# Gate and up projections as 2x2 blocks, every second chunk with seven products instead of eight

## The chip, the cores and the metric

One core of a Trainium2 chip runs the whole kernel. The metric is the device time of one execution in microseconds. The profile shows one such execution: TensorE as PE (matmuls) and PEld (its weight loads), VectorE as DVE, ScalarE as ACT, GpSimd as POOL, and the queue of SyncE, which issues most loads, as SPq.

## The reference

A decoder trunk of two layers over 256 tokens (two tiles of 128) and a model width of 2048, all in float32. Layer 0 mixes by retention and a short convolution, layer 1 by differential attention. After each mixer comes the feed-forward part, which is what the change touches:

```python
def swiglu(h, w_gate, w_up, w_down):
    return (jax.nn.silu(h @ w_gate) * (h @ w_up)) @ w_down
...
x = x + swiglu(rms_norm(x, norm_ffn[layer]), ffn_w_gate[layer], ffn_w_up[layer], ffn_w_down[layer])
```

`w_gate` and `w_up` are 2048 x 5632, `w_down` is 5632 x 2048. The gain of the norm is a column factor of `h`; its row scale `r` is applied to the products' results.

## The kernel before

Each float32 product is made of three products in a reduced format, fp32r. A matrix `a` is split in `a_hi` (rounded to fp32r) and `a_lo = a - a_hi`; then `a @ w` is `a_hi w_hi + a_lo w_hi + a_hi w_lo`. The activation stands still in TensorE (128 k-rows by 128 tokens), the weights move through it (128 k-rows by 512 columns), and one PSUM bank holds 128 tokens by 512 columns.

`col_block` (L126) makes one block of 512 columns for both token tiles. It loads the weights with SPq in pieces of four k-tiles, 1 MB each, into the tag `raw` (four buffers, L131), and goes through them in chunks of KC = 2 k-tiles: ScalarE makes `whi` (L138), VectorE `wlo` (L140), both of four buffers in the pool `wpool`, and TensorE runs 12 matmuls per chunk (2 token tiles x 2 k-tiles x 3, L146 to L148), each with its own weight load. A block over 16 k-tiles is 96 matmuls.

`ffn` (L398) runs three parts of 4, 4 and 3 column blocks. A block calls `col_block` for gate, lets ScalarE apply silu (L408), calls it for up, multiplies on VectorE (L411), and leaves a job that turns the hidden block for the down projection (`split4`, L158: four transposes on TensorE, `hi` on ScalarE at L165, `lo` on VectorE at L166). `step` (L114), called after every chunk, runs one piece of the oldest job, so jobs are spread through the next block. After each part, `out_proj` (L390) multiplies with the rows of `w_down` and adds to the residual `x_sb` (L228). There are 11 such gate and up pairs in each of the two layers, 22 in all.

`Stream` holds a norm's activation: `pair` (L184) turns two k-tiles of the residual and splits them (L197, L198); `part` runs it as a job while the projection ahead goes on.

The program's order and the tiles' dependencies are written out; `TileContext(nc, schedule_with_timeline_sim=True)` then fixes, before launch, the order of the instructions on each engine. Each engine runs its own list strictly in that order, waiting on semaphores. SPq and GpSimd's queue are two such lists.

Of the kernel before, what the change touches and what calls it, by code (L numbers as in the profile page):

```python
# [9 lines left out]
F32 = mybir.dt.float32  # L10
F32R = mybir.dt.float32r
# [24 lines left out]
def decoder_trunk(ctx: ExitStack, tc: tile.TileContext, a: dict):  # L36
# [16 lines left out]
    ident = cpool.tile([P, P], F32, name="ident")  # L53
    x_sb = cpool.tile([P, NT, D], F32, name="x_sb")
    gcol = cpool.tile([P, 88], F32, name="gcol")
# [48 lines left out]
    def rsqrt_mean(out, ss, n):  # L104
        """out = (ss / n + eps) ** -0.5 on small [P, w] tiles."""
        w = ss.shape[1]
        nc.vector.tensor_scalar(out, ss, 1.0 / n, EPS, ALU.mult, ALU.add)
        nc.gpsimd.tensor_tensor(out, out, mhalf[:, :w], ALU.pow)

    # Work that follows a product but holds the tensor engine runs between the chunks of the next  # L110
    # product: each job is a generator that yields where the tensor engine should go on meanwhile.
    jobs = deque()

    def step():  # L114
# [9 lines left out]
            step()  # L124

    def col_block(name, w, row0, n0, nk, hi, lo, kd=KD):  # L126
        """acc[t] = act[t] @ w[row0 : row0 + nk * P, n0 : n0 + NB], act split in hi + lo."""
        acc = [acc_tile(f"{name}_a{t}") for t in range(NT)]
        for c0 in range(0, nk, KC):
            if c0 % KD == 0:  # L130
                raw = wpool.tile([P, KD, NB], F32, tag="raw", name=f"{name}_raw{c0}", bufs=4)  # L131
# [19 lines left out]
        return acc  # L151

    def act_pair(nk, tag, name):
        hi = apool.tile([P, nk, S], F32R, tag=tag + "h", name=name + "_hi")
        lo = apool.tile([P, nk, S], F32R, tag=tag + "l", name=name + "_lo")
        return hi, lo

    def split4(src, hi, lo, k0, t, name):  # L158
        """Transpose src [P tokens, 512] of token tile t into k-tiles k0 .. k0+3 of hi and lo."""
        pt = tp_tile(f"{name}_tp")  # L160
        for j in range(4):
            nc.tensor.transpose(pt[:, j * P : (j + 1) * P], src[:, j * P : (j + 1) * P], ident)
        pv = pt.rearrange("p (j s) -> p j s", j=4)
        ts = slice(t * P, (t + 1) * P)
        nc.scalar.copy(hi[:, k0 : k0 + 4, ts], pv)  # L165
        nc.vector.tensor_tensor(lo[:, k0 : k0 + 4, ts], pv, hi.bitcast(F32)[:, k0 : k0 + 4, ts], ALU.subtract)  # L166

    class Stream:
        """The residual stream's next normed activation: x * gain, transposed and split, with
        the row scale kept apart for the products' results."""  # L170

        def __init__(self, name, g0):
            self.name, self.g0 = name, g0
            self.hi, self.lo = act_pair(KT, "xT", name)
            self.ss = small.tile([P, NT, 4], F32, tag="ss", name=name + "_ss")
            self.r = small.tile([P, NT], F32, tag="r", name=name + "_r")
# [5 lines left out]
                nc.scalar.activation(junk, x_sb[:, t, cs], AF.Square, accum_out=self.ss[:, t, c : c + 1])  # L182

        def pair(self, q):  # L184
            """k-tiles 2q and 2q + 1."""
            pt = tp_tile(f"{self.name}_tp{q}")
            for j in range(2):
                k = 2 * q + j
# [4 lines left out]
            for j in range(2):  # L193
# [5 lines left out]
                    self.lo[:, k], pv, g, self.hi.bitcast(F32)[:, k], op0=ALU.mult, op1=ALU.subtract  # L199
                )  # L200

        def scale(self):
            s1 = small.tile([P, NT], F32, tag="s1", name=self.name + "_s1")
            nc.vector.reduce_sum(s1, self.ss, axis=AX.X)
            rsqrt_mean(self.r, s1, D)

        def part(self, c):
            yield
            self.pair(2 * c)
            self.pair(2 * c + 1)  # L210
            yield
            self.squares(c)
            if c == 3:
                self.scale()
# [13 lines left out]
            nc.vector.tensor_tensor(x_sb[:, t, cs], acc[t], x_sb[:, t, cs], ALU.add)  # L228

    def rope(psum_in, r, cos, sin, out, h, hd, name):  # L230
        """out = rope(r * in) for h heads of hd columns; sin's first half carries the minus."""
        half = hd // 2
        v = psum_in.rearrange("p (h d) -> p h d", d=hd)
        ca = work.tile([P, h, hd], F32, tag="ropeA", name=name + "_A")
# [10 lines left out]
        nc.gpsimd.tensor_tensor(out.rearrange("p (h d) -> p h d", d=hd), ca, cb, ALU.add)  # L245

    def transpose4(src, dst, t, name):
        """src [P tokens, 512] -> dst[:, 0:4, tokens of t], float32."""
        pt = tp_tile(f"{name}_tp")
        for j in range(4):  # L250
            nc.tensor.transpose(pt[:, j * P : (j + 1) * P], src[:, j * P : (j + 1) * P], ident)
        nc.scalar.copy(dst[:, :, t * P : (t + 1) * P], pt.rearrange("p (j s) -> p j s", j=4))
# [136 lines left out]
    def out_proj(name, w, nk, hi, lo, g0, row0=0, stream=True):  # L389
        nxt = Stream(name, g0) if stream else None  # L390
        for c in range(4):
            acc = col_block(f"{name}o{c}", w, row0, c * NB, nk, hi, lo)
            add_residual(acc, c)
            if nxt:
                jobs.append(nxt.part(c))
        return (nxt, nxt.r) if nxt else None

    def ffn(layer, st, r, after):  # L398
        wg, wu, wd = a["ffn_w_gate"][layer], a["ffn_w_up"][layer], a["ffn_w_down"][layer]
        res = None  # L400
        for part, (b0, b1) in enumerate(((0, 4), (4, 8), (8, 11))):
            hi, lo = act_pair(KT, "act", f"h{layer}{part}")
            for b in range(b0, b1):
# [8 lines left out]
                jobs.append(splits(gs, hi, lo, 4 * (b - b0), f"h{layer}{b}"))  # L412
            nk, row0 = 4 * (b1 - b0), b0 * NB
            if part < 2:
                out_proj(f"d{layer}{part}", wd, nk, hi, lo, 0, row0, stream=False)
            elif after is not None:
# [53 lines left out]
    scale = AD ** -0.5  # L470

    def rotary(i, nm, acc, grp):
        """Norm and rotary embedding of four heads' q or k; returns both token tiles."""
        ct, sn = tabs[i]
        rots = []
        for t in range(NT):
# [174 lines left out]
```

## Time and profile before

| | us |
|---|---|
| median of three runs | 2235.31 (2234.86 to 2235.60) |
| span of the profiled execution, first to last instruction | 2233.8 |
| busy in it: TensorE, VectorE, ScalarE, GpSimd | 2224.0, 1235.7, 996.0, 115.8 |
| loaded and stored by DMA | 418.90 MB, 188 GB/s over the span |

The page gives no time of its own for the profiled execution beyond its span. The span ends 1.5 us short of the median of the runs, and this is what lies around it. A matmul's row lasts from its start to its modelled end, and the next one starts before that: time per matmul is read from start to start, not from the durations.

### The profile page before, as it was taken

How to read it: one execution, taken by the hardware profiler on the slowest of the kernel's cores; microseconds unless marked ns; L12 is line 12 of the kernel's file. 1: busy time of each engine (PE TensorE's matmuls, PEld its weight loads, DVE VectorE, ACT ScalarE, POOL GpSimd, SP SyncE). 2: the span in 40 equal slices, each digit the busy share in tenths (PEclk: the TensorE clock that was granted, in tenths of full speed). 3: DMA queues.
4: the chain of work that ended last, by engine and by line, in shares of the span. 5: the costliest groups of instructions: out<-in, count | busy, mean ns of one | idle time of the engine just before them, and what ended most of it. 6: DMA issues, size and time to landing. Idle time of an engine off the chain costs nothing.

```text
span 2233.8 us, 25353 instructions
## 1 busy us (share of the span) xinstructions
PE 2224.0 (100%) x10115; PEld 1842.8 (82%) x10115; DVE 1235.7 (55%) x1320; ACT 996.0 (45%) x1172; POOL 115.8 (5%) x104
## 2 busy tenths in 40 slices
PE   8999999999999999999999999999999999999999
PEld 7888888888888888888888888888888888888887
DVE  5555565544554555455677778665445544554554
ACT  5444445444334443444545545554444344434443
POOL 1110000000000000000031233000000000000000
PEclk9999999999999999999999999999999999999999
DMA  8555555555565655555555555555555656555553
GB/s 286 174 180 188 191 186 188 189 189 189 189 197 192 193 190 188 189 189 188 188 177 164 188 170 170 170 188 189 189 189 189 194 190 193 191 192 189 188 188 132
DMA packets 212860, 418.90 MB, mean 188 GB/s; under 512 B 7341, under 2 KB 10885, under 8 KB 212613
## 3 DMA queue, kind: packets, MB, share of 16 engines
q1 hardware_dynamic: 209904, 414.34, 56.7%
q10 hardware_dynamic: 2836, 2.93, 0.4%
q8 instruction: 79, 1.29, 0.2%
q14 instruction: 41, 0.33, 0.0%
HBM read 415.15 MB, written 2.10 MB: 187 GB/s over the span
## 4 chain that ended last, share of the span: by engine, by line
PE 99%; DMA 1%; ACT 0%; DVE 0%; SPq 0%; issue 0%
PE g_a L146 7%; PE g_a L148 7%; PE g_a L147 7%; PE u_a L146 7%; PE u_a L147 7%; PE u_a L148 7%; PE av_a L148 1%; PE av_a L146 1%; PE ak_a L148 1%; PE n3o_a L147 1%; PE ak_a L147 1%; PE n3o_a L146 1%; PE aq_a L147 1%; PE aq_a L148 1%; PE n3o_a L148 1%; PE n1o_a L148 1%
## 5 line engine op out<-in xcount | busy, mean ns | idle before, releaser
L140 DVE TENSOR_TENSOR u_lo<-u_raw,u_hi 128x1024 fp32r<-128x1024 f32 x176 | 215.6, 1225 | 263.0 <-ACT u_hi L138 263.0
L140 DVE TENSOR_TENSOR g_lo<-g_raw,g_hi 128x1024 fp32r<-128x1024 f32 x176 | 215.6, 1225 | 226.5 <-ACT g_hi L138 224.8
L138 ACT CAST g_hi<-g_raw 128x1024 fp32r<-128x1024 f32 x176 | 185.5, 1054 | 287.3 <-PE g_a L147 139.9
L138 ACT CAST u_hi<-u_raw 128x1024 fp32r<-128x1024 f32 x176 | 185.6, 1055 | 252.0 <-PE u_a L147 132.9
L146 PE MATMUL g_a<-g_hi,n_hi 128*128 128x512 f32 x704 | 277.3, 394 | 0.0
L148 PE MATMUL g_a<-g_lo,n_hi 128*128 128x512 f32 x704 | 274.4, 390 | 0.0
L147 PE MATMUL g_a<-g_hi,n_lo 128*128 128x512 f32 x704 | 273.9, 389 | 0.0
L146 PE MATMUL u_a<-u_hi,n_hi 128*128 128x512 f32 x704 | 273.9, 389 | 0.0
L147 PE MATMUL u_a<-u_hi,n_lo 128*128 128x512 f32 x704 | 273.9, 389 | 0.0
L148 PE MATMUL u_a<-u_lo,n_hi 128*128 128x512 f32 x704 | 273.9, 389 | 0.0
L148 PEld LDWEIGHTS g_a<-g_lo,n_hi 128*128 128x128 f32 x704 | 132.1, 188 | 28.1
L148 PEld LDWEIGHTS u_a<-u_lo,n_hi 128*128 128x128 f32 x704 | 132.2, 188 | 27.5
L146 PEld LDWEIGHTS u_a<-u_hi,n_hi 128*128 128x128 f32 x704 | 132.2, 188 | 27.4
L147 PEld LDWEIGHTS u_a<-u_hi,n_lo 128*128 128x128 f32 x704 | 132.2, 188 | 27.4
L147 PEld LDWEIGHTS g_a<-g_hi,n_lo 128*128 128x128 f32 x704 | 132.3, 188 | 26.5
L146 PEld LDWEIGHTS g_a<-g_hi,n_hi 128*128 128x128 f32 x704 | 132.2, 188 | 26.2
L140 DVE TENSOR_TENSOR d11o_lo<-d11o_raw,d11o_hi 128x1024 fp32r<-128x1024 f32 x32 | 39.2, 1225 | 42.2 <-ACT d11o_hi L138 42.1
L140 DVE TENSOR_TENSOR d00o_lo<-d00o_raw,d00o_hi 128x1024 fp32r<-128x1024 f32 x32 | 39.2, 1225 | 42.2 <-ACT d00o_hi L138 42.1
L140 DVE TENSOR_TENSOR d01o_lo<-d01o_raw,d01o_hi 128x1024 fp32r<-128x1024 f32 x32 | 39.2, 1225 | 42.2 <-ACT d01o_hi L138 42.1
L140 DVE TENSOR_TENSOR d10o_lo<-d10o_raw,d10o_hi 128x1024 fp32r<-128x1024 f32 x32 | 39.2, 1225 | 42.2 <-ACT d10o_hi L138 42.1
L140 DVE TENSOR_TENSOR n1o_lo<-n1o_raw,n1o_hi 128x1024 fp32r<-128x1024 f32 x32 | 39.4, 1232 | 35.6 <-ACT n1o_hi L138 35.6
L138 ACT CAST d10o_hi<-d10o_raw 128x1024 fp32r<-128x1024 f32 x32 | 33.8, 1055 | 53.3 <-PE d10o_a L147 46.6
(305 smaller groups left out, 4594.1 us busy)
## 6 DMA issues: line engine op xcount, KB each, us to landing
g_raw<-in_ffn_w_gate_dram SPq DMA_DIRECT2D x88, 1024.0 KB, 5.2
u_raw<-in_ffn_w_up_dram SPq DMA_DIRECT2D x88, 1024.0 KB, 5.2
n1o_raw<-in_hyb_w_out_dram SPq DMA_DIRECT2D x16, 1024.0 KB, 5.1
d00o_raw<-in_ffn_w_down_dram SPq DMA_DIRECT2D x16, 1024.0 KB, 5.1
d01o_raw<-in_ffn_w_down_dram SPq DMA_DIRECT2D x16, 1024.0 KB, 5.1
aq_raw<-in_diff_w_qkv_dram SPq DMA_DIRECT2D x16, 1024.0 KB, 5.1
ak_raw<-in_diff_w_qkv_dram SPq DMA_DIRECT2D x16, 1024.0 KB, 5.1
av_raw<-in_diff_w_qkv_dram SPq DMA_DIRECT2D x16, 1024.0 KB, 5.1
```

Source lines behind the costliest of these rows:

```text
L138: nc.scalar.copy(whi, part)
L140: nc.vector.tensor_tensor(wlo, part, whi.bitcast(F32), ALU.subtract)
L146: nc.tensor.matmul(acc[t], lhsT=hi[:, k, ts], rhs=whi[:, j], start=first, stop=False)
L147: nc.tensor.matmul(acc[t], lhsT=lo[:, k, ts], rhs=whi[:, j], start=False, stop=False)
L148: nc.tensor.matmul(acc[t], lhsT=hi[:, k, ts], rhs=wlo[:, j], start=False, stop=last)
```

## The change

Gate and up are computed together. The four k-tiles of a chunk are halves k1 and k2, the tokens are tiles t0 and t1, and gate and up are the two halves of the columns: a 2x2 block product. `pair_blocks` loads x (gate, four k-tiles) and y (up). In chunks 1 and 3 (kind 8) it makes eight half products of 6 matmuls; two of them use the difference of the two token tiles in place of one tile, so that the results land in the same banks. In chunks 0 and 2 (kind 7) it makes seven, of sums of blocks: an accumulating DMA issued by GpSimd adds the gate half w11 to the loaded up half w12 (that is t1), VectorE makes t2 = t1 + w22, t3 = t2 - w11 (in place of w11) and t4 = t2 + w21 (in place of w21), and all seven operands are split. The sums of the activation are made once per layer in `quad`. Seven PSUM banks hold the products; VectorE and ScalarE put gate and up together from them behind each pair. To make room, the transposes have one bank (`tpb`) instead of two while a pair runs, the working tiles live in a pool that is closed and opened again by stage (`Phase`), and `raw` has six buffers instead of four in the feed-forward stages.

```diff
+    class Phase:
+        def begin(self, name, raw):
+            if self.close is not None:
+                self.close.close()
+            self.close = ExitStack()
+            self.pool = self.close.enter_context(tc.tile_pool(name=name, bufs=2, reuse_waits="tile"))
+            self.raw = raw
...
+        def raw_tile(self, name):
+            return self.pool.tile([P, KD, NB], F32, tag="raw", name=name, bufs=self.raw)
...
     def tp_tile(name):
-        return psum.tile([P, NB], F32, tag="tp", name=name, bufs=2)
+        tp_turn[0] ^= 1
+        tag = "tpa" if tp_turn[0] and tp_both[0] else "tpb"
+        return psum.tile([P, NB], F32, tag=tag, name=name, bufs=1)
...
+    def split_w(src, name):
+        whi = wpool.tile([P, KC, NB], F32R, tag="whi", name=name + "_hi")
+        nc.scalar.copy(whi, src)
+        wlo = wpool.tile([P, KC, NB], F32R, tag="wlo", name=name + "_lo")
+        nc.vector.tensor_tensor(wlo, src, whi.bitcast(F32), ALU.subtract)
+        return whi, wlo
+
+    def pair_blocks(name, wa, wb, n0, st):
...
+        b7 = psum.tile([P, NB], F32, tag="tpa", name=f"{name}_p7", bufs=1)
+        b35 = psum.tile([P, 2, NB], F32, tag="sc", name=f"{name}_p35")
...
+        def product(c, bank, act, w, last=True):
+            hi, lo = act
+            whi, wlo = w
+            for j in range(KC):
...
+                nc.tensor.matmul(acc, lhsT=hi[:, j], rhs=whi[:, j], start=first, stop=False)
+                nc.tensor.matmul(acc, lhsT=lo[:, j], rhs=whi[:, j], start=False, stop=False)
+                nc.tensor.matmul(acc, lhsT=hi[:, j], rhs=wlo[:, j], start=False, stop=end)
+
+        for c, kind in enumerate(kinds):
+            k0 = c * KD * P
+            x = work.raw_tile(f"{name}_x{c}")
+            y = work.raw_tile(f"{name}_y{c}")
...
+            nc.sync.dma_start(x, wa[rows, cols].rearrange("(k p) n -> p k n", p=P))
+            nc.sync.dma_start(y, wb[rows, cols].rearrange("(k p) n -> p k n", p=P))
+            w11, w21, w12, w22 = x[:, 0:KC], x[:, KC:KD], y[:, 0:KC], y[:, KC:KD]
...
+            if kind == 7:
+                half = slice(k0, k0 + KC * P)
+                nc.gpsimd.dma_start(w12, wa[half, cols].rearrange("(k p) n -> p k n", p=P), accum_op=ALU.add)
+                t1 = w12
+                product(c, "b1", a["a11"], split_w(w11, nm + "w11"))
+                product(c, "b2", a["a12"], split_w(w21, nm + "w21"))
+                step()
+                t2 = work.tile([P, KC, NB], F32, tag="t2", name=nm + "t2", bufs=1)
+                nc.vector.tensor_tensor(t2, t1, w22, ALU.add)
+                nc.vector.tensor_tensor(w11, t2, w11, ALU.subtract)
+                nc.vector.tensor_tensor(w21, t2, w21, ALU.add)
+                product(c, "b6", a["s2"], split_w(t2, nm + "t2"))
+                product(c, "b7", a["s3"], split_w(w11, nm + "t3"))
+                step()
+                product(c, "b4", a["a22"], split_w(w21, nm + "t4"))
+                product(c, "b5", a["s1"], split_w(t1, nm + "t1"))
+                step()
+                product(c, "b3", a["s4"], split_w(w22, nm + "w22"))
+                if c == seven[-1]:
+                    u2 = work.tile([P, NB], F32, tag="u2", name=name + "u2", bufs=1)
+                    nc.scalar.copy(u2, b1)
+                    nc.vector.tensor_tensor(u2, b6, u2, ALU.subtract)
+                    u3 = work.tile([P, NB], F32, tag="u3", name=name + "u3", bufs=1)
+                    nc.vector.tensor_tensor(u3, b7, u2, ALU.add)
+            else:
+                w = split_w(w11, nm + "w11")
+                product(c, "b2", a["a11"], w, False)
+                product(c, "b4", a["a21"], w, False)
+                step()
...
+            step()
+        flush()
...
+        def quad(self, c):
...
+            nc.scalar.copy(self.hi[:, ks], xg)
+            nc.vector.tensor_tensor(self.lo[:, ks], xg, self.hi.bitcast(F32)[:, ks], ALU.subtract)
...
+            if n == 4:
+                nc.vector.tensor_tensor(d[:, 0], xg[:, k1, t1], xg[:, k2, t1], ALU.subtract)
+                nc.vector.tensor_tensor(d[:, 2], xg[:, k1, t1], xg[:, k1, t0], ALU.subtract)
+                nc.vector.tensor_tensor(d[:, 1], xg[:, k2, t1], d[:, 2], ALU.subtract)
+                nc.vector.tensor_tensor(d[:, 3], xg[:, k2, t0], d[:, 1], ALU.subtract)
+            else:
+                nc.vector.tensor_tensor(
+                    d.rearrange("p i k s -> p (i k) s"), xg[:, :, t0], xg[:, :, t1], ALU.subtract
+                )
...
+            nc.scalar.copy(hi, d)
+            nc.vector.tensor_tensor(lo, d, hi.bitcast(F32), ALU.subtract)
...
         def part(self, c):
             yield
-            self.pair(2 * c)
-            self.pair(2 * c + 1)
+            if self.kinds:
+                self.quad(c)
...
     def ffn(layer, st, r, after):
...
-                acc = col_block(f"g{layer}{b}", wg, 0, b * NB, KT, st.hi, st.lo)
+                b1, b2, b3, b4, b5, u2, u3 = pair_blocks(f"f{layer}{b}", wg, wu, b * NB, st)
...
+                nc.scalar.copy(gs[0], b1)
+                nc.vector.tensor_tensor(gs[0], b2, gs[0], ALU.add)
+                nc.vector.tensor_tensor(gs[1], b4, u3, ALU.subtract)
                 for t in range(NT):
-                    nc.scalar.activation(gs[t], acc[t], AF.Silu, scale=r[:, t : t + 1])
-                acc = col_block(f"u{layer}{b}", wu, 0, b * NB, KT, st.hi, st.lo)
-                for t in range(NT):
-                    nc.vector.scalar_tensor_tensor(gs[t], acc[t], r[:, t : t + 1], gs[t], op0=ALU.mult, op1=ALU.mult)
...
+                    nc.scalar.activation(gs[t], gs[t], AF.Silu, scale=r[:, t : t + 1])
+                nc.vector.tensor_tensor(u3, b5, u3, ALU.add)
+                nc.vector.tensor_tensor(u2, b5, u2, ALU.add)
+                nc.vector.tensor_tensor(u2, b3, u2, ALU.add)
+                for t, u in enumerate((u2, u3)):
+                    nc.vector.scalar_tensor_tensor(gs[t], u, r[:, t : t + 1], gs[t], op0=ALU.mult, op1=ALU.mult)
...
+    KINDS = (7, 8, 7, 8)
+    st, r = out_proj("n1", a["hyb_w_out"][0], KT, ca_hi, ca_lo, 32, kinds=KINDS, begin=("ffn0", 6))
     st, r = ffn(0, st, r, 16)
+    work.begin("mix1", 4)
```

`out_proj` calls `work.begin` behind its first column block where `begin` is given, so the pool changes at three places: in the projection ahead of each feed-forward part (`ffn0`, `ffn1`) and behind the first feed-forward part (`mix1`).

## Rows read from the trace of the kernel before

**Rows 1.** The page's first and second part: busy time, and tenths in 40 slices.

```profile
PE 2224.0 (100%) x10115; PEld 1842.8 (82%) x10115; DVE 1235.7 (55%) x1320; ACT 996.0 (45%) x1172; POOL 115.8 (5%) x104
...
PEclk9999999999999999999999999999999999999999
```

**Rows 2.** The chain that ended last, by engine and by line.

```profile
PE 99%; DMA 1%; ACT 0%; DVE 0%; SPq 0%; issue 0%
PE g_a L146 7%; PE g_a L148 7%; PE g_a L147 7%; PE u_a L146 7%; PE u_a L147 7%; PE u_a L148 7%; PE av_a L148 1%; PE av_a L146 1%; PE ak_a L148 1%; PE n3o_a L147 1%; PE ak_a L147 1%; PE n3o_a L146 1%; PE aq_a L147 1%; PE aq_a L148 1%; PE n3o_a L148 1%; PE n1o_a L148 1%
```

**Rows 3.** Timeline of TensorE: start us, duration us, line, operation; first pair of blocks.

```profile
405.10 0.39 PE L146 MATMUL u_a<-u_hi,n_hi 128*128 128x512 f32 x1
...
426.86 0.39 PE L146 MATMUL g_a<-g_hi,n_hi 128*128 128x512 f32 x1
...
432.07 0.39 PE L148 MATMUL g_a<-g_lo,n_hi 128*128 128x512 f32 x1
432.31 0.60 PE L162 MATMUL h_tp<-ident,gs 128*128 128x128 f32 x4
...
432.97 0.39 PE L147 MATMUL g_a<-g_hi,n_lo 128*128 128x512 f32 x1
```

**Rows 4.** Groups by line: engine, tile, shapes, count, busy us, mean ns, idle before.

```profile
L140 DVE TENSOR_TENSOR u_lo<-u_raw,u_hi 128x1024 fp32r<-128x1024 f32 x176 | 215.6, 1225 | 263.0 <-ACT u_hi L138 263.0
L138 ACT CAST u_hi<-u_raw 128x1024 fp32r<-128x1024 f32 x176 | 185.6, 1055 | 252.0 <-PE u_a L147 132.9 <-PE g_a L147 119.1
L411 DVE SCALAR_TENSOR_TENSOR gs<-u_a,n_r,gs 128x512 f32<-128x512 f32 x44 | 32.3, 748 | 0.0
L166 DVE TENSOR_TENSOR h_lo<-h_tp,h_hi 128x512 fp32r<-128x512 f32 x44 | 30.1, 683 | 0.0
L228 DVE TENSOR_TENSOR x_sb<-d00o_a,x_sb 128x512 f32<-128x512 f32 x8 | 5.5, 688 | 0.1
L408 ACT ACTIVATE gs<-g_a,n_r 128x512 f32<-128x512 f32 x44 | 30.2, 687 | 11.3 <-PE g_a L148 11.2
```

**Rows 5.** Busy by stretch: us, PE, PEld, DVE, ACT, POOL, PEclk, DMA share, GB/s.

```profile
0.00:40.00 40.00, 34.22 (x150) 26.88 (x151) 22.18 (x33) 24.61 (x46) 1.84 (x10) 1.00 0.93 324
...
382.00:560.00 178.00, 178.00 (x802) 147.50 (x801) 89.59 (x85) 78.31 (x86) 0.70 (x1) 1.00 0.59 190
```

**Rows 6.** Timeline of VectorE around a change of block; in brackets the idle time.

```profile
425.20 1.23 DVE L140 TENSOR_TENSOR g_lo<-g_raw,g_hi 128x1024 fp32r<-128x1024 f32 x1 [1.50 <-ACT g_hi L138]
426.34 1.47 DVE L411 SCALAR_TENSOR_TENSOR gs<-u_a,n_r,gs 128x512 f32<-128x512 f32 x2
427.92 1.23 DVE L140 TENSOR_TENSOR g_lo<-g_raw,g_hi 128x1024 fp32r<-128x1024 f32 x1
...
433.36 1.23 DVE L140 TENSOR_TENSOR g_lo<-g_raw,g_hi 128x1024 fp32r<-128x1024 f32 x1 [1.50 <-ACT g_hi L138]
434.50 0.68 DVE L166 TENSOR_TENSOR h_lo<-h_tp,h_hi 128x512 fp32r<-128x512 f32 x1
```

**Rows 7.** DMA issues: tile, queue, count, KB each, median us to landing.

```profile
g_raw<-in_ffn_w_gate_dram SPq DMA_DIRECT2D x88, 1024.0 KB, 5.2
...
rq_raw<-in_hyb_w_in_dram SPq DMA_DIRECT2D x8, 512.0 KB, 7.6
```

**Rows 8.** Timeline of VectorE in the attention layer, beside GpSimd's work.

```profile
1142.73 0.69 DVE L486 TENSOR_TENSOR aqsb<-aqsb,aqrr 128x512 f32<-128x512 f32 x1
1143.45 0.69 DVE L489 TENSOR_TENSOR aqA<-aqsb,rtab 128x512 f32<-128x512 f32 x1
1144.32 1.22 DVE L486 TENSOR_TENSOR aqsb<-aqsb,aqrr 128x512 f32<-128x512 f32 x1 [0.17 <-POOL aqrr L108]
1145.47 1.76 DVE L140 TENSOR_TENSOR ak_lo<-ak_raw,ak_hi 128x1024 fp32r<-128x1024 f32 x1
```

**Rows 9.** Timeline of GpSimd in the same stretch.

```profile
1144.26 4.71 POOL L491 TENSOR_TENSOR aqB<-aqsb,rtab 128x256 f32<-128x256 f32 x4
```

More of the change, by code (lines that the diff above doesn't have):

```diff
@@ L130, in col_block @@
             if c0 % KD == 0:
-                raw = wpool.tile([P, KD, NB], F32, tag="raw", name=f"{name}_raw{c0}", bufs=4)
+                raw = work.raw_tile(f"{name}_raw{c0}")
             if c0 % kd == 0:
@@ L151, in col_block @@
         return acc
+    def split_w(src, name):
[5 more added lines that the diff above has]
+    def pair_blocks(name, wa, wb, n0, st):
+        b1 = acc_tile(f"{name}_p1")
+        b2 = acc_tile(f"{name}_p2")
+        b6 = acc_tile(f"{name}_p6")
+        b4 = acc_tile(f"{name}_p4")
+        b7 = psum.tile([P, NB], F32, tag="tpa", name=f"{name}_p7", bufs=1)
+        b35 = psum.tile([P, 2, NB], F32, tag="sc", name=f"{name}_p35")
+        b3, b5 = b35[:, 0], b35[:, 1]
+        kinds = st.kinds
+        seven = [c for c, kind in enumerate(kinds) if kind == 7]
+        ends = {"b1": seven[-1], "b6": seven[-1], "b7": seven[-1]}
+        begun = set()
+        banks = {"b1": b1, "b2": b2, "b3": b3, "b4": b4, "b5": b5, "b6": b6, "b7": b7}
+        last_c = len(kinds) - 1
+        def product(c, bank, act, w, last=True):
+            hi, lo = act
+            whi, wlo = w
+            for j in range(KC):
+                first = bank not in begun
+                begun.add(bank)
+                end = last and j == KC - 1 and c == ends.get(bank, last_c)
+                acc = banks[bank]
+                nc.tensor.matmul(acc, lhsT=hi[:, j], rhs=whi[:, j], start=first, stop=False)
[5 more added lines that the diff above has]
+            y = work.raw_tile(f"{name}_y{c}")
+            rows = slice(k0, k0 + KD * P)
+            cols = slice(n0, n0 + NB)
+            nc.sync.dma_start(x, wa[rows, cols].rearrange("(k p) n -> p k n", p=P))
+            nc.sync.dma_start(y, wb[rows, cols].rearrange("(k p) n -> p k n", p=P))
+            w11, w21, w12, w22 = x[:, 0:KC], x[:, KC:KD], y[:, 0:KC], y[:, KC:KD]
+            a = st.blocks(c)
+            nm = f"{name}{c}"
+            if kind == 7:
[27 more added lines that the diff above has]
+                step()
+                w = split_w(w21, nm + "w21")
+                product(c, "b2", a["a12"], w)
+                product(c, "b4", a["a22"], w)
+                step()
+                w = split_w(w12, nm + "w12")
+                product(c, "b5", a["a21"], w, False)
+                product(c, "b3", a["d1"], w, False)
+                step()
+                w = split_w(w22, nm + "w22")
+                product(c, "b5", a["a22"], w)
+                product(c, "b3", a["d2"], w)
+            step()
+        flush()
+        return b1, b2, b3, b4, b5, u2, u3
@@ L200, in pair @@
                 )
+        def quad(self, c):
+            nm = f"{self.name}_c{c}"
+            xg = work.raw_tile(nm + "xg")
+            xg = xg.rearrange("p k n -> p (k n)")[:, 0 : KD * S].rearrange("p (k s) -> p k s", k=KD)
+            for q in range(2):
+                pt = tp_tile(f"{nm}_tp{q}")
+                for j in range(2):
+                    k = KD * c + 2 * q + j
+                    for t in range(NT):
+                        nc.tensor.transpose(
+                            pt[:, j * S + t * P : j * S + (t + 1) * P], x_sb[:, t, k * P : (k + 1) * P], ident
+                        )
+                for j in range(2):
+                    k = KD * c + 2 * q + j
+                    g = gcol[:, self.g0 + k : self.g0 + k + 1]
+                    nc.scalar.activation(xg[:, 2 * q + j], pt[:, j * S : (j + 1) * S], AF.Copy, scale=g)
+            ks = slice(KD * c, KD * c + KD)
+            nc.scalar.copy(self.hi[:, ks], xg)
+            nc.vector.tensor_tensor(self.lo[:, ks], xg, self.hi.bitcast(F32)[:, ks], ALU.subtract)
+            k1, k2, t0, t1 = slice(0, KC), slice(KC, KD), slice(0, P), slice(P, S)
+            n = 4 if self.kinds[c] == 7 else 2
+            d = work.raw_tile(nm + "sum")
+            d = d.rearrange("p k n -> p (k n)")[:, 0 : n * KC * P].rearrange("p (i k s) -> p i k s", i=n, k=KC)
+            if n == 4:
[6 more added lines that the diff above has]
+                    d.rearrange("p i k s -> p (i k) s"), xg[:, :, t0], xg[:, :, t1], ALU.subtract
+                )
+            hi = work.tile([P, n, KC, P], F32R, tag=f"sh{c}", name=nm + "_sh", bufs=1)
+            lo = work.tile([P, n, KC, P], F32R, tag=f"sl{c}", name=nm + "_sl", bufs=1)
+            nc.scalar.copy(hi, d)
+            nc.vector.tensor_tensor(lo, d, hi.bitcast(F32), ALU.subtract)
+            self.sums[c] = hi, lo
@@ new lines, in blocks @@
+        def blocks(self, c):
+            out = {}
+            for t in range(NT):
+                for h in range(2):
+                    ks, ts = slice(KD * c + KC * h, KD * c + KC * (h + 1)), slice(t * P, (t + 1) * P)
+                    out[f"a{t + 1}{h + 1}"] = self.hi[:, ks, ts], self.lo[:, ks, ts]
+            hi, lo = self.sums[c]
+            for i, nm in enumerate(("s1", "s2", "s3", "s4") if self.kinds[c] == 7 else ("d1", "d2")):
+                out[nm] = hi[:, i], lo[:, i]
+            return out
@@ L208, in part @@
             yield
-            self.pair(2 * c)
-            self.pair(2 * c + 1)
+            if self.kinds:
+                self.quad(c)
+            else:
+                self.pair(2 * c)
+                self.pair(2 * c + 1)
             yield
@@ L387, in decoder_trunk, with out_proj @@
         jobs.append(conv_out(half, cb))
[L389 to L390 removed]
+    def out_proj(name, w, nk, hi, lo, g0, row0=0, stream=True, kinds=None, begin=None):
+        nxt = Stream(name, g0, kinds) if stream else None
         for c in range(4):
@@ L393, in out_proj @@
             add_residual(acc, c)
+            if begin and c == 0:
+                work.begin(*begin)
             if nxt:
```

27 lines of the change are left out of this document (18 added, 9 removed).

## The prediction, made before the changed kernel ran

> **What bounds the kernel now.** I read the page's busy times first: TensorE is busy all through the span at a granted clock of full speed (2.4 GHz), VectorE 55%, ScalarE 45% [rows 1]. The chain that ended last runs through TensorE for 99% of the span, and six rows of 7% each, the gate and up matmuls, are 42% of it [rows 2]. So today only fewer or faster matmuls shorten the kernel, and the question is what takes over once some are gone.
>
> The pace of a matmul is read from starts. The first up matmul of a block starts at 405.10 and the next block's first at 426.86, 96 matmuls later [rows 3]: 21.76 / 96 = 0.2267 us. The four transposes of one `split4` cost 0.45 us more: from the last matmul ahead of them, 432.07, to the second behind them, 432.97, are 0.90 us where two matmuls take 0.45 [rows 3]. A pair of gate and up blocks thus takes 192 x 0.2267 + 2 x 0.45 = 44.4 us, and 22 pairs 977 us.
>
> VectorE does 16 splits of 1.225 us, two multiplies of 0.748 and two `h_lo` of 0.683 in a pair [rows 4]: 22.5 us of 44.4, about the half that the window of the first four pairs shows (89.6 of 178 us [rows 5]).
>
> **What is removed.** A seven-chunk has 7 x 6 = 42 matmuls for 48. Two of them per pair, 22 pairs: 44 x 6 = 264 matmuls x 0.2267 = **59.8 us**. They have the same shapes and weight loads, so I take the same pace. A pair then takes TensorE 180 x 0.2267 + 0.9 = 41.7 us. The other side of this number: one seven-chunk saves 1.36 us, and a wait of TensorE longer than that in each of them makes the kernel slower.
>
> **What is added on VectorE.** Per pair, in full durations:
> - Splits: 2 x 7 + 2 x 4 = 22 for 16, at 1.225 us: 26.9 us.
> - Block sums t2, t3, t4: six of 128x1024 with two SBUF inputs, the shape of the split, whose row I take: 7.4 us.
> - The seven adds that put gate and up together have one PSUM and one SBUF input of 128x512 (the last u2 add too); `x_sb` has that shape, 0.688 us [rows 4]: 4.8 us. Two multiplies 1.5, two `h_lo` 1.4.
>
> The sum is **42.0 us**, against TensorE's 41.7. But instructions that wait for nothing overlap at their ends: the split at 425.20 lasts 1.23 us and the next instruction starts at 426.34, 1.14 later; so again at 433.36 and 434.50 [rows 6]. With 0.09 us less for each of 39 instructions the sum is 38.5 us. VectorE's share is between 92% and 101% of TensorE's time, up from 51%. This closeness is what the forecast turns on. ScalarE has room: 22 copies of 1.055, two silu of 0.687, two PSUM copies and two `h_hi` taken at the same 0.687 [rows 4], 27.3 of 41.7 us.
>
> **How far VectorE runs ahead.** `whi` and `wlo` have four buffers, so at most four splits wait for TensorE. In an eight-chunk a split feeds 12 matmuls (2.72 us), in a seven-chunk 6 (1.36 us). From the release of a buffer to the split's end pass about 1.1 us on ScalarE and 1.2 on VectorE; four products of the seven-chunk last 5.44 us, so the cycle itself fits. In a seven-chunk VectorE's splits at 1.14 to 1.225 just keep step with 1.36; in an eight-chunk it must do one per 2.72 us and has 1.5 us free each time, about 6 us per eight-chunk: this is what the idle 263.0 us ahead of 176 `u_lo` is today [rows 4]. Into it must go the three sums of the next seven-chunk (3.7 us) and, in chunk 3, the u2, u3 and the two gs adds (2.8 us). They don't all fit, but splits in an eight-chunk have some microseconds of slack behind them. The scheduler already moves such work: `h_lo` ran behind the split of a later chunk and not at its place in the program [rows 6]. So I take these as covered.
>
> **The change of pair** is not covered. When b5 and b3 end, VectorE has three adds and two multiplies, 3 x 0.688 + 2 x 0.748 = 3.6 us, ahead of the fourth split of the new seven-chunk, which can't start earlier since its buffer has just come free. Three products are split, 4.08 us, and the fourth needs its `wlo` only in its third matmul, 0.45 later: 4.53. The split would end at 0.2 (an allowance for the matmul's tail, 0.39 against a pace of 0.23 [rows 3]) + 3.6 + 1.2 = 5.0: TensorE waits 0.5 us. In the same chunk come two `h_lo`, 1.4 us, against 0.14 to 0.22 us won per product: up to 0.6 more. I take 0.75 us per pair, 22 x 0.75 = **16.5 us**; the ends are 0 (everything overlaps) and 2 us per pair (full durations, 42.0, and 1.7 us in which VectorE has nothing to do while its buffers are full), 44 us.
>
> **The accumulating DMA.** No row of before shows one. It moves 512 KB, 1 MB per pair on top of 8 MB. Nearest rows: 1 MB lands in 5.2 us with the engines half idle, 512 KB in 7.6 us at the crowded start [rows 7]. Below, it is 2.6 us (half of 5.2); above, two crowded loads, since it also has to read what it adds to: 15.2 us. I take 7.6. It waits on GpSimd's queue for y, and there nothing else is queued during a pair; who waits for it is t2, and behind t2 everything on VectorE. With six `raw` buffers, x and y of a chunk are issued when those of three chunks earlier are split, some 25 us ahead of t2; two loads (10.4 us one behind the other) and 7.6 leave 7 us. Cost 0; if the cover goes, the price is that of the second rival. DMA bandwidth: 190 GB/s at a share of 0.59 now, 324 at 0.93 at the start [rows 5]; 9 MB in 41.7 us are 226 GB/s, a share near 0.7.
>
> **The rest.** `quad` adds a split of four k-tiles and sums with their split; all but the last of each layer run in `out_proj`, where VectorE has half its time free. The last falls into the first pair's chunk 0: 1.225 + 2 x 0.69 = 2.6 us, twice, and its transposes share one bank, so the second set waits for two copies, about 1 us. With both layers I take **5 us** (0 to 9). At three changes of pool, loads may start late; four splits of 2.72 us (10.9) cover a load of 5.2 and a split of 2.3: 0, at most 5.2 each.
>
> **Sum.** 2233.8 - 59.8 + 16.5 + 5 = 2195.5 for the span; with the 1.5 us that lie between the span and the median, **2197 us**.
>
> **One rule against it.** Beside a GpSimd instruction of 128x256 [rows 9], VectorE's 128x512 product took 1.22 us for 0.69 and a split 1.76 for 1.225 [rows 8]: 0.53 more each. The Trainium skill, "SBUF — State Buffer", section "Who interferes with whom", says that a VectorE instruction with two SBUF inputs contends with a GpSimd instruction that reads SBUF, and that the shared pair is an exclusive lock; that bears these rows out. It infers that writing DMA descriptors uses the other, writing interface; by that, an accumulating DMA would not touch the splits. No row here shows such a DMA.
>
> **Rivals.**
> 1. *VectorE sets the pace.* If little overlaps, a pair takes 42.0 us plus what VectorE idles at full buffers. At 1.4 us that is 43.4: 22 x (44.4 - 43.4) = 22 saved, 5 given back, 2218. For it: 101% at full durations. Against it: the overlap in the rows. Chance 0.15.
> 2. *The block sum comes late* (the slower side). If t1 lands only when TensorE enters the seven-chunk, just w11 and w21 are split (2.72 us); ahead of the next product are t2, t3, t4 and a split, 4 x 1.225 = 4.9 us (ScalarE's copy runs beside t3 and t4). TensorE waits at least 2.2 us, 44 times 97 us, for 60 saved: 2235 - 60 + 97 + 5 = 2277. It decides from 1.36 us of waiting on, that is from a landing some 14 us behind y. Against it: the 7 us of room. Chance 0.13.
> 3. *GpSimd's DMA issues hold VectorE.* 44 issues x 0.53 us, all on the path: 23 us, 2220. For it the rows in the attention layer, against it that nothing is known of an issue; the rule would make it nothing. Chance 0.07.
> 4. *Gain and waits cancel*, within 0.2% (4.5 us, about what the runs can tell): 0.03.
>
> **How the numbers follow.** The forecast has 0.62, with a range of its own from 2176 (no wait at all: 2235.3 - 59.8) to 2215 (1.5 us per pair). Faster: 0.62, most of rival 1 and of rival 3, 0.80. Same: rival 4 and the upper ends of 1 and 3, 0.06. Slower: 0.14, rival 2 and a little of 1. The range of 8 in 10 goes from 2176 to 2228; above it lie rival 2 and the ends of the others.
>
> **What would show it.** Right: 3960 gate and up matmuls at a pace of 0.227 us; pairs of about 42.4 us; VectorE above 85% in them; waits of TensorE on a `wlo`, in chunk 0 more than elsewhere; the accumulating DMA landed before t2's other releasers. Wrong: t2 waiting for a DMA in most seven-chunks (rival 2); splits longer than 1.3 us when GpSimd issues (rival 3); waits of TensorE spread evenly, with VectorE never idle (rival 1).

## The result, and the profile after

| | before | after |
|---|---|---|
| median, us | 2235.45 (2234.86 to 2235.67) | 2363.97 (2362.42 to 2364.95) |
| span of the profiled execution, us | 2233.8 | 2363.2 |

The ratio is 1.0574 (95% interval 1.0559 to 1.0589): 5.7% slower, where 1.7% faster was forecast. The forecast of 2197 us and its range up to 2228 are both missed, and the change goes the other way.

The page of the changed kernel: busy time, granted clock, the chain that ended last, and the DMA issues (KB each, median us to landing).

```profile
PE 2241.8 (95%) x9851; PEld 1820.1 (77%) x9851; DVE 1622.4 (69%) x1742; ACT 1158.0 (49%) x1362; POOL 170.4 (7%) x148
...
PEclk9999999999999999999999999899999999999999
...
PE 6%; DMA 2%; issue 0%; DVE 0%; ACT 0%; DVEq 0%; POOLq 0%
...
f_x<-in_ffn_w_gate_dram SPq DMA_DIRECT2D x88, 1024.0 KB, 5.4
f_y<-in_ffn_w_up_dram SPq DMA_DIRECT2D x88, 1024.0 KB, 6.1
f_y<-in_ffn_w_gate_dram POOLq DMA_DIRECT2D x44, 512.0 KB, 6.0
```

The matmuls that were to go are gone: 10115 - 9851 = 264 [rows 1]. Yet TensorE is busy longer, 2241.8 us for 2224.0. The loss can be split by the page's busy and idle time. Without the 264 matmuls at the old pace it would be 2224.0 - 59.8 = 2164.2 us busy; it is 77.6 more. And its idle time grew from 9.8 us (2233.8 - 2224.0) to 121.4 (2363.2 - 2241.8), by 111.6. So 77.6 + 111.6 - 59.8 = 129.4 us, the difference of the spans: the saving came, and waits and slower matmuls took it three times over. The chain of before lay on TensorE for 99% [rows 2]; here it can be followed back through a small part of the span only, so the waits have to be read one by one.

What TensorE waited for in all of the span (us in total, times, longest), five of the rows, each of the last two standing for many like it in other pairs:

```profile
PE n3o_a L172 <- ACT n3o_hi L164: 12.9, 3, 4.6
PE n1o_a L172 <- ACT n1o_hi L164: 12.8, 3, 4.5
PE f_p L212 <- DVE x_sb L401: 7.8, 4, 2.9
...
PE f_p L214 <- DVE f082t_lo L183: 4.0, 1, 4.0
...
PE f_p L212 <- DVE f02u L590: 2.1, 1, 2.1
```

There are two places: the pairs, where TensorE waits for splits and sums of VectorE, and the two projections `n1o` and `n3o`, where no matmul was changed. The windows below answer to [rows 5], over the first four pairs (columns as there): VectorE is busy for 155 of 194 us, 80%. It is not the bound by its load, so what it waited for is the question. The second row is 3.7 us behind one wait of TensorE.

```profile
401.00:594.70 193.70, 178.77 (x753) 141.76 (x753) 154.95 (x155) 107.25 (x120) 9.12 (x8) 0.96 0.66 206
...
508.84:512.50 3.66, 3.66 (x9) 2.89 (x10) 3.66 (x4) 0.51 (x1) 0.00 (x0) 0.53 0.37 93
```

The idle time of VectorE ahead of t2 (L235), by what ended it (us, times):

```profile
its engine sat idle before it (us, times) until:
  DMA f_y<-in_ffn_w_gate_dram: 78.3, 19
  issue: 68.4, 22
```

Here are 146.7 us, in 41 of the 44 seven-chunks. Timelines of one of them show how it comes about. First VectorE, from just behind the last split of chunk f021 on; t2 of pair 3's chunk 0 is `f030t`:

```profile
517.31 0.68 DVE L284 TENSOR_TENSOR h_lo<-h_tp,h_hi 128x512 fp32r<-128x512 f32 x1
...
527.20 1.22 DVE L183 TENSOR_TENSOR f022t_lo<-f_x,f022t_hi 128x1024 fp32r<-128x1024 f32 x1 [1.34 <-ACT f022t_hi L181]
531.01 1.23 DVE L235 TENSOR_TENSOR f030t<-f_y 128x1024 f32<-128x1024 f32 x1 [2.59 <-DMA f_y<-in_ffn_w_gate_dram]
532.15 1.22 DVE L183 TENSOR_TENSOR f022t_lo<-f_x,f022t_hi 128x1024 fp32r<-128x1024 f32 x1
...
541.83 1.22 DVE L183 TENSOR_TENSOR f030w_lo<-f_x,f030w_hi 128x1024 fp32r<-128x1024 f32 x1 [0.45 <-ACT f030w_hi L181]
```

Then the issue of `y` of that chunk on SPq, and that of the accumulating DMA on GpSimd:

```profile
517.42 0.37 SPq L223 DMA_DIRECT2D f_y<-in_ffn_w_up_dram  x1
```

```profile
500.08 1.19 POOL L229 DMA_DIRECT2D f_y<-in_ffn_w_gate_dram  x1 [21.91 <-DVE f_x L237]
525.03 1.19 POOL L229 DMA_DIRECT2D f_y<-in_ffn_w_gate_dram  x1 [23.75 <-DMA f_y<-in_ffn_w_up_dram]
```

The buffer of `y` comes free when the splits of f021 end, `y` is issued at 517.42, GpSimd starts the accumulation at 525.03, and t2 starts at 531.01: 13.6 us from the free buffer to t1. That is no long time, and chunk f030 gets its first split only at 541.83. But in VectorE's list t2 of f030 stands among the splits of chunk f022, one chunk and a half ahead of its use, and whatever stands behind it there waits with it: the split at 532.15 is one that TensorE needs at once (the row at 533.42 below). Where the row says "issue", the same DMA is behind it: `f022t` starts at 506.20 with 2.73 us of such idle time ahead, 6.1 us behind GpSimd's issue at 500.08, and 6.0 us is the median time to landing. (That it was this DMA is read from the times; e2 below bears it out.)

The timeline of TensorE just there shows the second half of the loss:

```profile
508.84 0.56 PE L212 MATMUL f_p<-f020t_hi,n_c_sh 128*128 128x512 f32 x1 [1.90 <-DVE f01u L590]
509.19 0.63 PE L213 MATMUL f_p<-f020t_hi,n_c_sl 128*128 128x512 f32 x1
509.62 0.63 PE L212 MATMUL f_p<-f021w_hi,n_hi 128*128 128x512 f32 x1
...
512.57 0.40 PE L213 MATMUL f_p<-f021w_hi,n_lo 128*128 128x512 f32 x1
512.80 0.39 PE L214 MATMUL f_p<-f020t_lo,n_c_sh 128*128 128x512 f32 x1
...
533.42 0.50 PE L214 MATMUL f_p<-f022t_lo,n_hi 128*128 128x512 f32 x1 [0.66 <-DVE f022t_lo L183]
```

What ended the wait of 1.90 us is the sum `f01u`, and in VectorE's list it stood behind `f022t`:

```profile
506.20 1.23 DVE L235 TENSOR_TENSOR f022t<-f_y 128x1024 f32<-128x1024 f32 x1 [2.73 <-issue]
...
508.01 0.68 DVE L590 TENSOR_TENSOR f01u<-f_p,f01u 128x512 f32<-128x512 f32 x1
```

Behind 1.90 us of idle time matmuls start 0.43 us apart (509.19 to 509.62) for some 3.5 us, then 0.23 again (512.57 to 512.80). The granted clock of that stretch is 0.53, the 1.2 GHz level for nearly all of it. So this wait is paid twice, once as idle time and once in the matmuls behind it. Not every wait is: behind that of 0.66 us at 533.42 the granted clock stays at 1.00 (window 533.4 to 540.0), and of the changed kernel's 14 waits of 1.9 to 2.6 us, six were followed by a granted clock of 1.00, of the 14 longer ones none.

### The profile page after: what moved, and what is told of

The parts are those of the page before. It is cut to its first block, busy times and chain, and to the rows that moved or that the text cites. A ratio compares the mean times of both kernels' runs of the same rounds, so it can differ in the third digit from the quotient of the medians.

```text
span 2363.2 us, 25883 instructions
## 1 busy us (share of the span) xinstructions
PE 2241.8 (95%) x9851; PEld 1820.1 (77%) x9851; DVE 1622.4 (69%) x1742; ACT 1158.0 (49%) x1362; POOL 170.4 (7%) x148
## 5 line engine op out<-in xcount | busy, mean ns | idle before, releaser
L229 POOL DMA_DIRECT2D f_y<-in_ffn_w_gate_dram x44 | 53.1, 1207 | 1565.0 <-DMA f_y<-in_ffn_w_up_dram 761.4
L172 PE MATMUL n3o_a<-n3o_hi,oT_hi 128*128 128x512 f32 x128 | 54.0, 422 | 12.9 <-ACT n3o_hi L164 12.9
L172 PE MATMUL n1o_a<-n1o_hi,cat_hi 128*128 128x512 f32 x128 | 53.2, 415 | 12.8 <-ACT n1o_hi L164 12.8
L166 DVE TENSOR_TENSOR aq_lo<-aq_raw,aq_hi 128x1024 fp32r<-128x1024 f32 x32 | 39.3, 1232 | 26.1 <-ACT aq_hi L164 26.0
L173 PE MATMUL n3o_a<-n3o_hi,oT_lo 128*128 128x512 f32 x128 | 53.5, 418 | 0.0
L166 DVE TENSOR_TENSOR n3o_lo<-n3o_raw,n3o_hi 128x1024 fp32r<-128x1024 f32 x32 | 38.4, 1222 | 21.1 <-ACT n3o_hi L164 21.0
L173 PE MATMUL n1o_a<-n1o_hi,cat_lo 128*128 128x512 f32 x128 | 52.3, 408 | 0.0
L174 PE MATMUL n3o_a<-n3o_lo,oT_hi 128*128 128x512 f32 x128 | 51.4, 417 | 0.0
L172 PE MATMUL aq_a<-aq_hi,d0b_hi 128*128 128x512 f32 x128 | 50.4, 394 | 0.8 <-ACT aq_hi L164 0.8
L166 DVE TENSOR_TENSOR ak_lo<-ak_raw,ak_hi 128x1024 fp32r<-128x1024 f32 x32 | 39.9, 1248 | 16.1 <-ACT ak_hi L164 16.1
```

Source lines behind the costliest of these rows:

```text
L229: nc.gpsimd.dma_start(w12, wa[half, cols].rearrange("(k p) n -> p k n", p=P), accum_op=ALU.add)
```

## The experiments

All were compared with the kernel before on the same chip (medians 2235.21 to 2235.35).

**e1: t2 in its turn.** The sum t2 is tied to stand behind the last split of the chunk ahead of it. The computation and the DMAs stay.

```diff
+            behind = last_split[0]   # VectorE's newest split, of the chunk ahead
...
-                nc.vector.tensor_tensor(t2, t1, w22, ALU.add)
+                with tc.issue_after(behind.ins) if behind is not None else ExitStack():
+                    nc.vector.tensor_tensor(t2, t1, w22, ALU.add)
```

> The sum t2 is put on VectorE's list behind the last split of the chunk ahead of it; nothing else is changed. Theory A (VectorE's list has t2 of the next seven-chunk too early, among the splits of the present one, and VectorE stands still there until the accumulating DMA lands: 147 us ahead of 41 of the 44 t2 in the changed kernel): the waits ahead of t2 fall to under 20 us in all, the waits of TensorE go with them, and the time to 2190 to 2230 us. Theory B (VectorE's load itself is the bound, 101% at full durations): the waits only move to other places, and the time stays above 2320. Theory C (the accumulating DMA or its issue slows other work): no change, about 2364.

Measured: 2248.93 us, ratio 1.0058 (1.0043 to 1.0073). One place in a list gives back 115.0 of the 128.5 us lost (besides the sums only neighbours change places: 1642 of VectorE's 1742 instructions run in the same order as in the changed kernel). That is neither B nor C, but it is 19 us above the range of theory A: the projections' waits stay, and they are the subject of e5. VectorE's idle time ahead of t2 falls to 22.1 us in 7 cases, a little over the 20 expected. TensorE's waits that remain, by the same view, are those of the projections, unchanged, and little in the pairs:

```profile
PE n3o_a L172 <- ACT n3o_hi L164: 12.9, 3, 4.6
PE n1o_a L172 <- ACT n1o_hi L164: 12.8, 3, 4.5
...
PE f_p L214 <- ACT f001w_hi L183: 1.6, 1, 1.6
```

**e2: no accumulation.** The accumulating DMA is left out, so t1 is w12 alone and the output is not the reference's; t2 stands as early as in the changed kernel, and the sums and splits are all done.

```diff
-                nc.gpsimd.dma_start(w12, wa[half, cols]..., accum_op=ALU.add)
```

> Leaves out the accumulating DMA, so t1 is only the up half and the result is not the reference's; VectorE's list has the sums at the same places. Theory A: t2 finds its input loaded, the waits ahead of it go, 2190 to 2230 us. Theory B: above 2320. Theory C: as A, so that e1 tells A from C.

Measured: 2248.19 us, ratio 1.0056 (1.0039 to 1.0072), and 1.3 us of VectorE's idle time ahead of t2; the range of theory A is missed as in e1. With e1 this settles the first cause: the place alone (e2) and the DMA alone (e1, which is 0.7 us slower than e2 with all 44 x 512 KB accumulated) cost about nothing; an early place and an operand that lands late cost 115 us together. In both, the third and fourth pair take 42.3 us each, as in e6 below, where TensorE has no wait in the pairs.

**e3, e4: the block sum without DMA.** t1 is made in SBUF by VectorE (e3) or by GpSimd (e4).

```diff
-                nc.gpsimd.dma_start(w12, wa[half, cols]..., accum_op=ALU.add)
+                nc.vector.tensor_tensor(w12, w12, w11, ALU.add)      # e3
+                nc.gpsimd.tensor_tensor(w12, w12, w11, ALU.add)      # e4
```

> The sum t1 is made by VectorE in place of the accumulating DMA: 44 more instructions of 1.2 us, so VectorE's load in a pair goes from 38.5 to 42.0 us to 40.7 to 44.4, against 41.7 of TensorE. Theory A: faster than 2364 though VectorE does more, since it waits for no accumulation: 2220 to 2270. Theory B: slower than the changed kernel by up to 54 us, 2380 to 2420.

> The sum t1 is made by GpSimd from the loaded halves: by its rows in the attention layer (four of 128x256 in 4.7 us) some 5 us per sum, against 7.2 us from issue to landing of the accumulating DMA. Theory A: a little less waiting ahead of t2, but VectorE's instructions beside it are longer by 0.53 us each, four or five of them per sum: 2300 to 2370. Theory B: more load on VectorE, above 2380.

Measured: e3 2258.25 us, ratio 1.0104 (1.0089 to 1.0119); e4 2278.41 us, 1.0194 (1.0178 to 1.0209). On VectorE the 44 adds, about 50 us of its time at 1.14 each, cost 10.1 us over e2: most of them go where it has time, in line with the 91% shown below. On GpSimd the sum is 30.2 us dearer than nothing; 2278.41 us lies below the range of either theory. (The 7.2 us for the accumulating DMA were misread: from issue to landing it is 6.0.) Part of the 30.2 is an idle VectorE ahead of t2 (55.9 us in 28 cases, ended by GpSimd), part are longer instructions: of the 44 VectorE instructions of 128x1024 that run beside one of these adds, 14 last over 1.3 us. VectorE in e4:

```profile
494.53 1.22 DVE L237 TENSOR_TENSOR f_x<-f020t,f_x 128x1024 f32<-128x1024 f32 x1
495.67 3.44 DVE L183 TENSOR_TENSOR f020t_lo<-f020t,f020t_hi 128x1024 fp32r<-128x1024 f32 x1
```

and GpSimd in e4:

```profile
495.34 2.69 POOL L229 TENSOR_TENSOR f_y<-f_y,f_x 128x1024 f32<-128x1024 f32 x1 [17.52 <-DMA f_y<-in_ffn_w_up_dram]
```

The split that starts beside GpSimd's add takes 3.44 us for 1.22.

**e5: own tiles for quad.** In the feed-forward pools `quad`'s two working tiles were two of the six `raw` buffers; now they use the room of t2 and gs, which is idle in the projections.

```diff
-            xg = work.raw_tile(nm + "xg")
+            xg = work.tile([P, KD, S], F32, tag="t2", name=nm + "xg", bufs=1)
...
-            d = work.raw_tile(nm + "sum")
+            d = work.tile([P, n, KC, P], F32, tag="gs", name=nm + "sum", bufs=1)
```

> In quad the two tiles xg and sum take the tags t2 and gs (idle then) in place of two of the six raw buffers; t2 stays at its early place on VectorE's list. Theory D (in the projections ahead of the feed-forward parts, quad's tiles hold raw buffers until transposes that come late, so loads and splits of the next block start late: the two projections take 110 and 122 us for 90 and 94 before): these two fall to under 100 each, 40 to 55 us less than the changed kernel, 2309 to 2324, with the waits ahead of t2 as they were. Theory E (quad's own work on ScalarE and VectorE, in order, holds the projection): less than 12 us.

Measured: 2309.77 us, ratio 1.0329 (1.0312 to 1.0345), 54.2 us less than the changed kernel, with 145.7 us of idle time ahead of t2 as before. By the timelines, the stretch from the first matmul of `n1o` to the first of `d00` goes from 303.7 to 277.8 us, that from `n3o` to `d10` from 317.4 to 288.9: 54.4 us of the 61.8 by which the two profiled executions differ (2363.2 and 2301.4). Of it 39.7 us lie in the projections themselves, which now take 90.8 and 102.6 us (the second was expected under 100), and the rest in the first pairs behind them. What happened there is best seen in e1, where nothing else disturbs. ScalarE, then TensorE:

```profile
319.88 1.57 ACT L341 ACTIVATE n_c0xg<-n_c_tp,gcol 128x256 f32<-128x256 f32 x4 [4.43 <-PE n_c_tp L335]
...
323.69 3.88 ACT L164 CAST n1o_hi<-n1o_raw 128x1024 fp32r<-128x1024 f32 x4
```

```profile
319.79 0.49 PE L335 MATMUL n_c_tp<-ident,x_sb 128*128 128x128 f32 x3
324.79 0.80 PE L172 MATMUL n1o_a<-n1o_hi,cat_hi 128*128 128x512 f32 x1 [4.50 <-ACT n1o_hi L164]
325.38 0.63 PE L173 MATMUL n1o_a<-n1o_hi,cat_lo 128*128 128x512 f32 x1
```

ScalarE stands idle for 4.43 us until the transposes of `quad` are there, with four splits of the projection queued behind them; TensorE then has nothing for 4.50 us. That happens at three of the four column blocks of each projection, 25.7 us of waits, and the granted clock of the stretch behind this one, 324.8 to 330.8, is 0.51: matmuls at 0.43 us again. From e1 to e6, where this is mended, TensorE's idle time falls by 32.8 us (47.0 to 14.2) and its busy time by 22.1 (2200.9 to 2178.8).

Theory D had the number, but the loads were not what these splits waited for. The two pieces that the four splits at 323.69 read were issued on SPq at 305.29 and 305.71 and landed 5.3 and 7.6 us later, at 310.6 and 313.3, ten microseconds and more before (e1; the two issues with their durations in ns, and the time to landing in us, each as lowest, median and highest):

```profile
L161 SPq DMA_DIRECT2D n1o_raw<-in_hyb_w_out_dram x2: 368/434/499, 305.3 to 305.7; - x2
DMA to landing us min/median/max: 5.3/6.4/7.6
```

What held them was their place in ScalarE's list, behind `quad`'s copies. With the two buffers given back that list comes out otherwise, as e6 shows below; how the buffers led to the order was not tried.

**e6: both edits, e1 and e5.**

> e1 and e5 together. If the two causes are apart and complete: 2249 less 40 to 55 us, 2194 to 2209, near the 2197 forecast for the change. Theory E: 2237 to 2249.

Measured: **2195.65 us**, ratio 0.9823 (0.9808 to 0.9837), 1.8% faster than the kernel before. The two effects add up: 2363.97 - 115.0 - 54.2 = 2194.8. Its page:

```profile
PE 2178.8 (99%) x9851; PEld 1795.2 (82%) x9851; DVE 1624.6 (74%) x1742; ACT 1158.6 (53%) x1362; POOL 172.3 (8%) x148
...
PE 99%; DMA 1%; DVE 0%; ACT 0%; issue 0%; SPq 0%; ACTq 0%; POOL 0%; DVEq 0%
PE f_p L214 14%; PE f_p L216 14%; PE f_p L215 14%; PE n3o_a L173 1%; PE n3o_a L172 1%; PE aq_a L174 1%; PE n3o_a L174 1%; PE d11o_a L174 1%; PE av_a L174 1%; PE av_a L173 1%; PE av_a L172 1%; PE ak_a L174 1%; PE ak_a L173 1%; PE n1o_a L172 
```

The chain lies on TensorE again, as in [rows 2], and its list of waits has none in the pairs. The window over the first four pairs, from 3 us behind their start on (columns as in [rows 5]):

```profile
385.00:551.20 166.20, 166.20 (x741) 136.18 (x740) 150.79 (x148) 104.57 (x115) 7.86 (x7) 1.00 0.73 224
```

VectorE is 91% busy, at a DMA share of 0.73 and 224 GB/s. Its timeline in e6, t2 now behind the last split of chunk f023, and a split while GpSimd issues:

```profile
487.36 1.22 DVE L185 TENSOR_TENSOR f022t_lo<-f022t,f022t_hi 128x1024 fp32r<-128x1024 f32 x1
...
499.94 1.23 DVE L185 TENSOR_TENSOR f023w_lo<-f_y,f023w_hi 128x1024 fp32r<-128x1024 f32 x1 [0.30 <-ACT f023w_hi L183]
501.08 1.22 DVE L239 TENSOR_TENSOR f030t<-f_y 128x1024 f32<-128x1024 f32 x1
502.22 1.22 DVE L185 TENSOR_TENSOR f030w_lo<-f_x,f030w_hi 128x1024 fp32r<-128x1024 f32 x1
```

```profile
487.27 1.19 POOL L232 DMA_DIRECT2D f_y<-in_ffn_w_gate_dram  x1 [21.29 <-DMA f_y<-in_ffn_w_up_dram]
```

And ScalarE in the projection of e6, where the splits of `n1o` stand between `quad`'s copies instead of behind them:

```profile
319.60 1.05 ACT L164 CAST n1o_hi<-n1o_raw 128x1024 fp32r<-128x1024 f32 x1 [1.68 <-PE n1o_a L173]
320.56 1.57 ACT L340 ACTIVATE n_c0xg<-n_c_tp,gcol 128x256 f32<-128x256 f32 x4
...
323.20 1.05 ACT L164 CAST n1o_hi<-n1o_raw 128x1024 fp32r<-128x1024 f32 x1
```

**e7, e8: how many seven-chunks.** Both are e6 with another list of kinds: e7 has none, so no sums of the weights, no accumulation, and a shorter end of a pair (written anew for it, lines not shown); e8 has three of four.

```diff
-    KINDS = (7, 8, 7, 8)
+    KINDS = (8, 8, 8, 8)    # e7
+    KINDS = (7, 7, 7, 8)    # e8
```

> e6 with eight products in every chunk: no seven-chunk, no block sums, no accumulating DMA, a shorter end of pair, the same pools, banks and pairing. It shows what the seven products themselves bring. By the pace of 0.2267 us the 264 matmuls are 59.8 us, less the waits at the change of pair that e1 still has (0.5 us per pair): e7 45 to 60 us above e6, 2245 to 2265. If the seven products bring nothing because VectorE is full: within 15 us of e6.

> e6 with three seven-chunks of four: 132 matmuls less (30 us of TensorE), and per pair three splits and three sums more on VectorE: 45.4 us at overlapped, 49.4 at full durations, against 40.4 of TensorE. Theory B for this load (VectorE sets the pace as soon as its sum passes TensorE's): 22 x (45.4 to 49.4 less some 42.2) = 70 to 158 us above e6, 2265 to 2360, VectorE busy above 95% in the pairs. If VectorE's load is not a bound: 30 us below e6.

Measured: e7 2251.95 us, ratio 1.0074 (1.0059 to 1.0089); e8 2264.63 us, 1.0133 (1.0116 to 1.015), 0.4 us under the range of theory B. Against e7 the 44 seven-chunks of e6 bring 56.3 us, of the 59.8 reckoned. Pairing gate and up without them costs 16.7 us. e8 has 132 matmuls fewer than e6 and is 69.0 us slower. Its window over the first four pairs, cut as before:

```profile
385.00:567.10 182.10, 169.80 (x717) 131.61 (x716) 175.96 (x172) 115.46 (x128) 11.31 (x10) 0.98 0.70 214
```

VectorE is busy for 176 of 182 us. From its first matmul to that of the next, a pair takes 45.2 to 45.4 us in e8 and 42.3 in e6 (fifth to eighth pair, without the first behind the down block, which lacks the transposes). Six VectorE instructions more at 1.14 on top of 38.5 are 45.3, at full durations 42.0 + 7.4 = 49.4: the overlapped durations were the right ones, and VectorE becomes the bound with the third seven-chunk, not with the second.

## Why the prediction was wrong

**Right.** 264 matmuls went, and their value was 56.3 us for 59.8. VectorE's load, put at 92% to 101% of TensorE's time with the lower end taken, is 91% in e6, and a pair takes 42.3 us for 42.4. DMA was put at 226 GB/s and 0.7, and is at 224 and 0.73. The accumulating DMA was priced at 7.6 us between 2.6 and 15.2, and lands 6.0 us after its issue. The sum, 2197 us, is what e6 takes to within 1.4 us: the arithmetic of the loads described a kernel that was not the one given. That it comes so close is in part luck: the 16.5 and 5 us that it adds to the saving are 19.0 in e6 (2193.0 - 2233.8 + 59.8), but not from what they were put down to, as shown below.

**The first step that failed** is "The accumulating DMA", with its "Cost 0" from "some 25 us ahead of t2". The 25 us were counted with t2 at its place in the program, behind the first two products of its chunk. In the list of VectorE it stands one chunk and a half earlier: its turn comes at 528.4 (527.20 + 1.22), 11.0 us behind the issue of `y`, and t1 needs 13.6. I had the fact that should have warned me, and used it for the other side: under "How far VectorE runs ahead", "The scheduler already moves such work ... So I take these as covered". A list that can move `h_lo` later can put a sum earlier than its operand. Rival 2 had the right effect, t2 late and everything behind it on VectorE late, and I gave it 0.13; but it places the wait where TensorE enters the seven-chunk with t1 not landed, and priced it at 2.2 us, 44 times, 97 us. In truth t1 was in time for its own chunk; what was held up were the splits and sums of the chunk before. The price, 115.0 us by e1, is 2.6 us per seven-chunk, idle time and slower matmuls together. I had not counted the clock: in no row of before does TensorE wait in the pairs.

**The second** is "The rest": "all but the last of each layer run in `out_proj`, where VectorE has half its time free", 5 us (0 to 9). VectorE's time was not what `quad` needed. It took two of six `raw` buffers, and with that its copies stood ahead of the projection's splits in ScalarE's list, waiting for transposes; giving the buffers back won 54.2 us by e5. I counted its instructions, and neither their place in the list nor the buffers. Without this fault, the projection `n1o` takes 90.8 us in e6 for 90.7 before, so nothing of a late load at the change of pool shows there either.

**The change of pair**, 16.5 us of waits, is mis-sized in kind: with both causes gone TensorE has no wait there at all. What a pair takes above the 41.7 us is some 0.5 us (42.27 for 44.47 - 12 x 0.2267 = 41.75, both over the first four pairs), 11 us in 22 pairs, in matmuls that start a little later one behind the other. The timelines show which: in the first four pairs of e6, those with one of `quad`'s sums standing in TensorE follow each other at 0.232 us (median), all others at 0.227; in e7, without a sum of the weights, it is the same 0.232 and 0.227, and a pair takes 44.8 us for 44.5. So a full VectorE is not needed for it, and why these matmuls are slower stays open. Some 6 us more lie between `n3o` and `d10`, where e6 takes 270.5 us for 272.9 - 4 x 2.7 = 262.1 (2 us of that are the four pairs' own). TensorE waits 3.0 and 1.2 us at the end of the attention there, in e7 too, and matmuls follow at a granted clock of 0.54; why the attention ends with a wait now was not tried and stays open. So does why the list has t2 so early: the runs show that it does and what it costs.

**The other rivals.** Rival 1 is wrong for two seven-chunks and right for three (e8). Rival 3 is wrong: the split at 487.36 in e6 takes 1.22 us while GpSimd issues for 1.19 from 487.27, and of the 67 VectorE instructions of 128x1024 that run beside one of the 44 issues none lasts over 1.23 us. The inference of the Trainium skill, "SBUF — State Buffer", section "Who interferes with whom", that such an issue needs another interface than a VectorE instruction with two SBUF inputs reads through, agrees with these rows, and its rule that a GpSimd instruction reading SBUF does contend agrees with the 3.44 us of e4.

## What to carry to other kernels

An instruction that needs a late operand costs what stands behind it in its engine's list, so look for it where the list has it and not where the program has it; if that place can't be known before, don't put its cost at nothing. When a new step enters a stage and borrows its buffers, ask also which ready work will stand behind the step in each list, besides how long its own instructions are. And price a wait of TensorE of some microseconds at more than its length, since behind most of those here the matmuls ran at half the pace.

## What the runs showed of the hardware

A 512 KB accumulating DMA took 1.2 us of GpSimd's time and landed 6.0 us (median of 44) after its issue, beside plain 1 MB loads at 5.4 and 6.1. Waits of TensorE of 1.90 and 4.50 us were followed by matmuls 0.43 us apart, 3.7 and 6.0 us long, nearly all of it at the 1.2 GHz level (granted clock 0.53 and 0.51); of the changed kernel's 14 waits of 1.9 to 2.6 us, six were followed by a granted clock of 1.00, of the 14 longer ones none. A GpSimd add of 128x1024 made a VectorE split beside it 3.44 us long for 1.22 (14 of 44 VectorE instructions beside such adds were longer than 1.3 us), and a DMA issue by GpSimd left it at 1.22. Matmuls with a sum of `quad` standing in TensorE followed each other at 0.232 us for 0.227.
